# State-space constants: the input table built transposed from a host-transposed B, short-kernel products in four column groups, order and paces reset

## The chip, the cores and the metric

The kernel runs on one core of one Trainium2 chip. The metric is device microseconds of one execution. The kernel before took 1513.43 us, the median of 3 runs (1512.66 to 1515.32).

## The reference

One decoder block: a sequence of 1040 positions (16 learned meta positions and 1024 tokens) of width 1024, float32 throughout.

```python
p     = h @ w_in + b_in            # [u_s5 | q | k | v | o | i | f | g_s5 | g_m]
y_s5  = GLU(GELU(S5(u_s5)))        # grouped complex-diagonal state space
y_m   = (o * HeadNorm(mLSTM(q, k, v, i, f))) @ m_w_out
mix   = sigmoid(g_s5) * y_s5 + sigmoid(g_m) * y_m
h     = LN(alpha * h + mix @ w_o)
h     = LN(alpha * h + relu(h @ w_up + b_up)^2 @ w_down)
...
def _s5_mixer(u, lam_re, lam_im, log_dt, b_re, b_im, c_re, c_im, d_skip):
    lam_bar = jnp.exp(lam * dt)                       # 32 groups x 64 states, complex
    b_bar = ((lam_bar - 1.0) / lam)[..., None] * b_mat
    bu = jnp.einsum("gph,blgh->blgp", b_bar, u)       # 16 inputs per group
    _, state = lax.associative_scan(_linear_recurrence_combine, (a, bu), axis=1)
    y = jnp.real(jnp.einsum("ghp,blgp->blgh", c_mat, state))
    return y + d_skip * u
```

## The kernel before

**Tiling and jobs.** The projection is cut into jobs, one per block of columns of `w_in`, run in the order of the string `ORDER` (`q`/`k`, `v`, `u` for the state space, `o`, and pairs of gate blocks in two parts, `a` and `b`), and then eight `glu` and eight `ym` jobs; the output projection and the feed-forward stage come after all of these. A float32 product is made of three products of rounded parts (`whi`/`wlo` for weights, `hT_hi`/`hT_lo` for activations, lines L262 to L264 in `mm3`); the split is one ScalarE copy (`whi`) and one VectorE subtraction (`wlo`, L243).

**Lanes.** Everything that is not a projection is written as generators: the mLSTM (`ml`), the state-space constants (`s5c`) and batches (`s5`), its GELU (`s5g`), the preparation of gate and up weights (`hg`, `up`), the reload of `hT` (`ah`). After every second term, `mm3` advances a modelled clock (`pump`), and a lane runs on once its last `yield`, times its `PACE`, is past. The lists `ML`, `NL`, `C5`, `K5`, `Z5`, `D5`, `W5` and `Y5` are such yields, for each head or batch. This gives each instruction its place; the scheduler then fixes the order on each engine. All big tiles share one pool of 30 slots, and the small products share three PSUM buffers (`sdps`).

**mLSTM.** Four heads of nine chunks. Per chunk: `pk` (transpose, L517), `pS` (L522, then `sw` on VectorE, L524), `pn` (L532 and L533, numerator and denominator, which reads the state `C`), `pu` (L536, the update, added to `C` on VectorE at L541, copied at L539 for the first chunk), and the normalisation with `dd` (L551 to L554) and `hst`/`hmv`.

**State space.** Chunks of 8 positions, 32 groups, handled in four batches of eight groups. `s5_pre` starts at the job `S5_START` and makes `lam_bar`, its powers `E` (and `ER`, the same in reversed order), the factor `wr`, `wi` and from it `bb`, and the rotation table. When a `u` job ends, it stores `u` to DRAM (L612) and adds two generators. `s5_consts` (for batch b):

- six GpSimd products (L777 and on) of `bb` and `ER` into the table `s5P`, with partitions over states;
- six VectorE operations of `C` and `E` into `s5Rr`, `s5Ri`, and a block-diagonal copy of `bb` beside it;
- eight TensorE transposes of `s5P` (L814) and two ScalarE copies into `s5Mi` (L815), the weights of the input product;
- the short kernel (the response within a chunk): eight products of 32 columns of weights with 128 moving columns (L821, L822), all into partitions 0 to 31 of one PSUM buffer, copied to `s5Kt` (32 x 512), with the skip term added by four small VectorE operations (L826);
- `s5RS` by GpSimd copies; `s5Mx` cleared and filled by 16 DMAs from `s5Kt`, SBUF to SBUF (L839); the table `s5T` by rotation.

`s5_batch` loads `s5U` (eight DMAs, L860), waits for the constants, makes the input products `s5z` (L876), a scan on VectorE in three sets of operations that end with `s5w` (L920), and the output products `s5y`, alternately from `s5Mx` (L931) and from `s5RS` and `s5w` (L932). Loads and stores of this part go through SP's queue, in the order of the program.

**Other places the text speaks of.** The head output `hmF` (L578); the split of gate weights `gmwh` and `gmwl` (L992, L993); the gate sums `hgr` (L970); the stored partial results `gme` (L1152); the reload of a part of `hT` through `ttr` by ScalarE and VectorE (L1103, L1104), with its preparation `tpr` (L1082). `up_early` makes the first up weights and stores them in `wu_dr`. The gate pairs whose `b` part is among the first three (`HOLD`) of `ORDER` and whose `a` part is among the last three keep their weights in SBUF (`HELD`); the others go to DRAM (`gw_dr`, `e_dr`) and come back.

## Time and profile before

The profiled execution is known by its span alone, 1511.4 us from the first to the last instruction; the median of the runs shown is 1513.43.

| engine | busy share of 40 equal slices, in tenths |
|---|---|
| PE | 9999999999999999999999999999999999999997 |
| DVE | 7677756787978785575876676666666689767786 |
| ACT | 7634542425345654241352244444444524433340 |
| POOL | 0000001523104000000000011000000000000000 |
| PE clock | 9999999999999999999999999999999999999999 |
| DMA | 9504362406748678898872257544443997767642 |

A digit is the busy share of one slice of 37.8 us, 9 standing for 90% or more. PE is TensorE's matmuls, PEld its weight loads, DVE VectorE, ACT ScalarE, POOL GpSimd, SP the engine that issues most DMAs. The state-space constants are made in the slices where GpSimd is busy, roughly 230 to 480 us. The core moves 307.06 MB in all, at 203 GB/s.

A row of grouped instructions names line, engine, operation, output and inputs, the count, and then the shortest, median and longest (or total and mean) time of one. A row of the chain or the timeline begins with its start and its length in us. A row of waits names who waited, for whom, and the sum, count and longest.

### The profile page before, as it was taken

The page shows a single profiled execution, that of the slowest core. Times are in us where ns is not written, and L with a number is a line of the kernel's source. Part 1 is how long each engine was busy: PE and PEld are TensorE (multiplying, and loading weights), DVE is VectorE, ACT ScalarE, POOL GpSimd, SP SyncE. Part 2 cuts the span into 40 slices and gives each one's busy share as a digit, 9 for nine tenths or more (in the row PEclk, how much of TensorE's full clock was granted, in tenths as well). Part 3 has the DMA queues.
Part 4 walks back from the last instruction along what each step waited for, and adds up shares of the span by engine and source line. Part 5 has one row for each costly group of instructions (what it writes and reads, how often), then busy time and mean ns, then how long its engine had stood idle before and what let it go on. Part 6 is the DMA issues. An engine that isn't in the chain of part 4 may idle for free.

```text
span 1511.4 us, 20671 instructions
## 1 busy us (share of the span) xinstructions
PE 1495.8 (99%) x7564; PEld 1265.8 (84%) x7564; DVE 1074.7 (71%) x1983; ACT 635.8 (42%) x989; POOL 95.2 (6%) x170
## 2 busy tenths in 40 slices
PE   9999999999999999999999999999999999999997
PEld 9999989998788788888888888888888888888886
DVE  7677756787978785575876676666666689767786
ACT  7634542425345654241352244444444524433340
POOL 0000001523104000000000011000000000000000
PEclk9999999999999999999999999999999999999999
DMA  9504362406748678898872257544443997767642
GB/s 328 156 14 135 110 198 88 145 5 179 247 142 284 184 280 323 342 384 338 340 281 84 71 188 232 180 152 153 144 144 124 313 381 269 241 224 240 205 178 101
DMA packets 150644, 307.06 MB, mean 203 GB/s; under 512 B 19640, under 2 KB 62080, under 8 KB 150544
## 3 DMA queue, kind: packets, MB, share of 16 engines
q1 hardware_dynamic: 147456, 294.68, 56.6%
q0 software_dynamic: 3024, 11.01, 2.3%
q8 instruction: 59, 0.97, 0.3%
q14 instruction: 41, 0.34, 0.1%
q10 hardware_dynamic: 64, 0.07, 0.0%
HBM read 201.63 MB, written 102.90 MB: 201 GB/s over the span
## 4 chain that ended last, share of the span: by engine, by line
PE 93%; DVE 2%; DMA 2%; ACT 1%; POOL 1%; issue 1%; SPq 0%; DVEq 0%; POOLq 0%; ACTq 0%
PE mm L262 22%; PE mm L264 22%; PE mm L263 22%; PE sd L262 6%; PE sd L263 6%; PE sd L264 6%; PE mm L258 2%; DMA wraw<-in_wf_dram 1%; PE pu L536 1%; PE pn L532 1%; PE mm L297 1%; PE pn L533 1%; PE s5y L932 0%; DMA ttr<-t_dr 0%; PE ln L1621 0%
## 5 line engine op out<-in xcount | busy, mean ns | idle before, releaser
L262 PE MATMUL mm<-hT_hi,whi 128*128 128x512 f32 (+3 forms) x400 | 147.7, 369 | 0.0
L264 PE MATMUL mm<-hT_hi,wlo 128*128 128x512 f32 (+3 forms) x400 | 145.5, 365 | 0.0
L263 PE MATMUL mm<-hT_lo,whi 128*128 128x512 f32 (+3 forms) x400 | 144.9, 362 | 0.0
L263 PE MATMUL sd<-dwl,dah 128*128 128x512 f32 (+1 forms) x256 | 98.9, 386 | 0.0
L262 PE MATMUL sd<-dwh,dah 128*128 128x512 f32 (+1 forms) x256 | 98.8, 387 | 0.0
L264 PE MATMUL sd<-dwh,dal 128*128 128x512 f32 (+1 forms) x256 | 98.6, 386 | 0.0
L1829 ACT ACTIVATE dah<-da 128x1024 fp32r<-128x1024 f32 x56 | 58.6, 1052 | 90.6 <-PE sd L263 39.9
L1833 ACT ACTIVATE dwh<-wdr 128x1024 fp32r<-128x1024 f32 x56 | 58.9, 1053 | 77.9 <-DMA wdr<-in_wdn_dram 27.5
L1830 DVE TENSOR_TENSOR dal<-da,dah 128x1024 fp32r<-128x1024 f32 x56 | 68.2, 1220 | 23.1 <-ACT dah L1829 22.8
L262 PEld LDWEIGHTS mm<-hT_hi,whi 128*128 128x128 f32 x400 | 75.2, 188 | 9.7 <-issue 0.3
L263 PEld LDWEIGHTS mm<-hT_lo,whi 128*128 128x128 f32 x400 | 75.2, 188 | 9.3 <-issue 0.3
L264 PEld LDWEIGHTS mm<-hT_hi,wlo 128*128 128x128 f32 x400 | 75.2, 188 | 9.1
L263 PE MATMUL mm<-dwl,dah 128*128 128x512 f32 (+1 forms) x208 | 80.1, 386 | 0.0
L262 PE MATMUL mm<-dwh,dah 128*128 128x512 f32 (+1 forms) x208 | 80.0, 386 | 0.0
L264 PE MATMUL mm<-dwh,dal 128*128 128x512 f32 (+1 forms) x208 | 79.9, 385 | 0.0
L262 PE MATMUL mm<-hT_hi,gmwh 128*128 128x512 f32 x192 | 77.1, 404 | 1.7 <-ACT gme L1152 1.2
L263 PE MATMUL mm<-hT_lo,gmwh 128*128 128x512 f32 x192 | 75.9, 395 | 0.0
L1834 DVE TENSOR_TENSOR dwl<-wdr,dwh 128x1024 fp32r<-128x1024 f32 x56 | 68.2, 1220 | 9.8 <-ACT dwh L1833 9.1
L264 PE MATMUL mm<-hT_hi,gmwl 128*128 128x512 f32 x192 | 74.8, 396 | 0.0
L262 PE MATMUL mm<-whi,hT_hi 128*128 128x256 f32 (+1 forms) x256 | 74.3, 290 | 0.0
L264 PE MATMUL mm<-whi,hT_lo 128*128 128x256 f32 (+1 forms) x256 | 73.9, 289 | 0.0
L263 PE MATMUL mm<-wlo,hT_hi 128*128 128x256 f32 (+1 forms) x256 | 73.6, 288 | 0.0
(492 smaller groups left out, 3967.5 us busy)
## 6 DMA issues: line engine op xcount, KB each, us to landing
da<-act_dr SPq DMA_DIRECT2D x56, 512.0 KB, 5.1
wdr<-in_wdn_dram SPq DMA_DIRECT2D x56, 512.0 KB, 5.5
wraw<-in_wf_dram SPq DMA_DIRECT2D x36, 512.0 KB, 5.9
wur<-in_wup_dram SPq DMA_DIRECT2D x32, 512.0 KB, 4.4
act_dr<-upy SPq DMA_DIRECT2D x64, 256.0 KB, 2.6
wu_dr<-wpre SPq DMA_DIRECT2D x21, 512.0 KB, 4.8
wpre<-wu_dr POOLq DMA_DIRECT2D x21, 512.0 KB, 4.7
act_dr<-upx SPq DMA_DIRECT2D x32, 256.0 KB, 3.4
```

What stands on the lines that cost most here:

```text
L258: t_.matmul(ps, tm[i], tm[j], start=(w == 0 and k == 0), stop=(w == 2 and k == n - 1))
L262: t_.matmul(ps, ah, bh, start=(i == 0 and part[0]), stop=False, skip_group_check=skip)
L263: t_.matmul(ps, ah, bl, start=False, stop=False, skip_group_check=skip)
L264: t_.matmul(ps, al, bh, start=False, stop=(i == n - 1 and part[1]), skip_group_check=skip)
L297: t_.matmul(ps[:, :P], job.first[:, k * P:(k + 1) * P], HF[c0 // P][:, k * P:(k + 1) * P], start=(k == 0), stop=(k == KT - 1))
L532: t_.matmul(pn[:, :257], qi[:, c0:c0 + n], Cs[c][:, :257], start=True, stop=False)
L533: t_.matmul(pn[:, :257], sws[c], vt[c][:, :257], start=False, stop=True)
L536: t_.matmul(pu[:, :257], kws[c][:n], vt[c][:n, :257], start=True, stop=True)
L1829: a_.activation(ah[:, :D], a[:, :D], AF.Copy)
L1830: v_.tensor_tensor(alo[:, :D], a[:, :D], f32(ah[:, :D]), op=OP.subtract)
L1833: a_.activation(wh, raw[i], AF.Copy)
L1834: v_.tensor_tensor(wl, raw[i], f32(wh), op=OP.subtract)
```

## The change

**The input table.** The host passes B a second time, transposed and repeated eight times, so that its partitions are (position in the chunk, input) and its columns (group, state): `s5bt`. `s5_pre` makes the powers times the factor (`WE`, eight powers), transposes these two 128 x 128 blocks once, and stores them in DRAM (`we_dr`). For each batch, `s5_in_load` loads the batch's part of `s5bt` (512 KB, `s5BT`) and, with eight DMAs that repeat a row over 16 partitions, the powers (`s5WT`); four VectorE products and two sums give `s5Mi` in the layout in which TensorE needs it. The six GpSimd products, `ER`, the eight transposes and the two ScalarE copies of each batch are gone.

**The short kernel.** The eight products go to four column groups (partitions 0 to 31, 32 to 63, 64 to 95, 96 to 127), the four of the real part first and then the four of the imaginary part. `s5Kt` is 128 x 128; the skip term is one VectorE operation. It is stored in DRAM (`kt_dr`) and read back into `s5Mx` by eight DMAs.

**Order and paces.** `ORDER`, `S5_START`, `LANE_AT`, `TPW`, `PACE` and seven of the lists of yields have other values. In `ORDER` the `b` parts begin with 11, 10 and 5, so gate pair 9 isn't held in SBUF.

```diff
-ORDER = 'q0 q1 v0 v1 q3 q2 o1 o3 o0 v2 o2 u0 u1 v3 o5 u2 o7 o4 a5 a6 a4 o6 u3 a7 a8 a11 a10 a9 b10 b11 b9 b5 b8 b6 b4 b7'
+ORDER = 'q0 q1 v0 v1 q3 q2 o3 o1 v2 o2 u0 u1 v3 o0 o7 o5 u2 o4 o6 a4 a6 a5 u3 a7 a8 a11 a10 a9 b11 b10 b5 b9 b8 b6 b4 b7'
-TPW = 10.0
-S5_START = 'o2'
-LANE_AT = {'t_prep': 'q3', 'hm_gate': 'b9', 'ah_scale': 'glu2', 'up_early': 'ym2'}
-PACE = {'ml': 0.56, 'cv': 0.093, 's5': 1.0, 's5c': 0.722, 's5g': 2.2, 'ah': 1.569, 'up': 1.036, 'hg': 3.426}
+TPW = 9.77
+S5_START = 'q3'
+LANE_AT = {'t_prep': 'q1', 'hm_gate': 'b9', 'ah_scale': 'glu2', 'up_early': 'ym3'}
+PACE = {'ml': 0.448, 'cv': 0.116, 's5': 1.0, 's5c': 0.65, 's5g': 2.2, 'ah': 1.569, 'up': 1.295, 'hg': 3.426}
-ML = [2.875, 1.694, 2.242, 5.174]
-NL = [0.292, 2.653, 1.274, 3.476]
-C5 = [1.146, 1.058, 1.99, 0.152]
-K5 = [0.475, 9.599, 1.568, 8.674]
+ML = [2.875, 1.694, 2.646, 5.174]
+NL = [0.292, 1.327, 1.274, 6.604]
+C5 = [2.292, 1.058, 1.99, 0.179]
+K5 = [0.475, 9.877, 2.195, 8.674]
-D5 = [3.696, 1.28, 0.645, 0.254]
-W5 = [3.774, 0.829, 4.498, 0.851]
-Y5 = [2.738, 0.964, 2.648, 4.789]
+D5 = [3.696, 1.28, 1.29, 0.254]
+W5 = [3.774, 0.829, 5.308, 0.851]
+Y5 = [2.738, 1.147, 3.707, 4.789]
...
-        dtl = mid.tile([32, 16], F32, name="s5_d")
+        dtl = mid.tile([P, 4], F32, name="s5_d")
-        eye = mid.tile([32, 16], F32, name="s5_eye")
+        eye = mid.tile([P, 16], F32, name="s5_eye")
-        v_.tensor_tensor(eye, ident[:32, 0:16], ident[:32, 16:32], op=OP.add)
+        v_.tensor_reduce(eye, ident.rearrange("p (m h) -> p h m", h=16), axis=mybir.AxisListType.X, op=OP.add)
...
-        ER = es[:, 288:544].rearrange("p (r e q) -> p r e q", r=2, q=16)
+        WE = es[:, 288:544].rearrange("p (r e q) -> p r e q", r=2, q=16)
-        S5.update(E=E, ER=ER, r8=r8)
...
+        yield 1.3
+        sh = [P, 8, 16]
+        cmul(v_, WE[:, 0], WE[:, 1], E[:, 0, 0:8], E[:, 1, 0:8],
+             wr[:, None, :].to_broadcast(sh), wi[:, None, :].to_broadcast(sh),
+             tm[:, 0:128].rearrange("p (a b) -> p a b", b=16), tm[:, 256:384].rearrange("p (a b) -> p a b", b=16))
+        yield 1.3
+        ps = sdps("s5p")
+        for ri in range(2):
+            t_.transpose(ps[:, ri * P:(ri + 1) * P], es[:, 288 + ri * P:288 + (ri + 1) * P], ident)
+        wet = slot("s5wt")
+        a_.activation(wet[:, 0:256], ps[:, 0:256], AF.Copy)
+        nc.sync.dma_start(we_dr.rearrange("p r c -> p (r c)"), wet[:, 0:256])
...
+    we_dr = dram.tile([P, 2, P], F32, name="we_dr")
+    kt_dr = dram.tile([4, P, P], F32, name="kt_dr")
+    def s5_in_load(b):
+        bt, wt = slot("s5BT"), slot("s5WT")
+        nc.sync.dma_start(bt[:, 0:1024], s5bt[:, b])
+        for j in range(8):
+            nc.sync.dma_start(wt[16 * j:16 * j + 16, 0:1024],
+                              bass.AP(tensor=we_dr.tensor, offset=we_dr.offset + ((7 - j) * 16 + 4 * b) * 256,
+                                      ap=[[0, 16], [1, 1024]]))
+        return bt, wt
-        E, ER = S5["E"], S5["ER"]
+        E = S5["E"]
+        bt, wt = s5_in_load(b)
...
-        Pt, tm = slot("s5P"), slot("s5tm")
-        sh = [P, 4, 8, 16]
-        br, bi = (B4(r)[:, :, None, :].to_broadcast(sh) for r in (0, 1))
-        er, ei = (E4(ER, r)[:, :, :, None].to_broadcast(sh) for r in (0, 1))
-        t1, t2 = v4(tm[:, 0:512]), v4(tm[:, 512:1024])
-        pr, pi = v4(Pt[:, 0:512]), v4(Pt[:, 512:1024])
-        g_.tensor_tensor(t1, br, er, op=OP.mult)
-        g_.tensor_tensor(t2, bi, ei, op=OP.mult)
-        yield C5[b]
-        g_.tensor_tensor(pr, t1, t2, op=OP.subtract)
-        g_.tensor_tensor(t1, br, ei, op=OP.mult)
-        yield C5[b]
-        g_.tensor_tensor(t2, bi, er, op=OP.mult)
-        g_.tensor_tensor(pi, t1, t2, op=OP.add)
-        yield C5[b]
-        Mi, Kt = slot("s5Mi"), slot("s5Kt")[:32, :512]
-        for ri in range(2):
-            ps = sdps("s5p")
+        Mi, tm = slot("s5Mi"), slot("s5tm")
+        def v5(t):
+            return t[:, 0:1024].rearrange("p (q r c) -> p q r c", q=4, r=2)
+        def m5(r):
+            return Mi[:, 0:1024].rearrange("p (q g r n) -> p q g r n", q=4, g=2, r=2)[:, :, :, r, :]
+        def t5(r):
+            return v5(tm)[:, :, r, :].rearrange("p q (g n) -> p q g n", g=2)
+        v_.tensor_tensor(tm[:, 0:1024], bt[:, 0:1024], wt[:, 0:1024], op=OP.mult)
+        yield C5[b]
+        v_.tensor_tensor(m5(0), t5(0), t5(1), op=OP.subtract)
+        yield C5[b]
+        v_.tensor_tensor(v5(tm)[:, :, 0], v5(bt)[:, :, 0], v5(wt)[:, :, 1], op=OP.mult)
+        v_.tensor_tensor(v5(tm)[:, :, 1], v5(bt)[:, :, 1], v5(wt)[:, :, 0], op=OP.mult)
+        yield C5[b]
+        v_.tensor_tensor(m5(1), t5(0), t5(1), op=OP.add)
+        yield C5[b]
+        Kt = slot("s5Kt")[:, :P]
+        ps = sdps("s5k")
+        for ri, R in ((0, Rr), (1, Ri)):
-                t_.transpose(ps[:, q * P:(q + 1) * P], Pt[:, ri * 512 + q * P:ri * 512 + (q + 1) * P], ident)
-            a_.activation(Mi[:, 0:1024].rearrange("p (g r s) -> p g r s", g=8, r=2)[:, :, ri, :],
-                          ps.rearrange("p (g s) -> p g s", g=8), AF.Copy)
-            yield C5[b]
-        ps = sdps("s5k")
-        for q in range(4):
-            o = ps[:32, q * P:(q + 1) * P]
-            t_.matmul(o, Rr[:, 576 + q * 32:576 + q * 32 + 32], Rr[:, q * 144:q * 144 + P], start=True, stop=False)
-            t_.matmul(o, Rr[:, 704 + q * 32:704 + q * 32 + 32], Ri[:, q * 144:q * 144 + P], start=False, stop=True)
-        a_.activation(Kt, ps[:32, :], AF.Copy)
-        for q in range(4):
-            k0 = Kt[:, q * P:q * P + 16]
-            v_.scalar_tensor_tensor(k0, S5["eye"], S5["d"][:, q0 + q:q0 + q + 1], k0, op0=OP.mult, op1=OP.add)
+                w0 = 576 + 128 * ri + 32 * q
+                t_.matmul(ps[32 * q:32 * q + 32, 0:P], Rr[:, w0:w0 + 32], R[:, q * 144:q * 144 + P],
+                          start=(ri == 0), stop=(ri == 1))
+        a_.activation(Kt, ps[:, 0:P], AF.Copy)
+        v_.scalar_tensor_tensor(Kt[:, 0:16], S5["eye"], S5["d"][:, b:b + 1], Kt[:, 0:16], op0=OP.mult, op1=OP.add)
+        nc.sync.dma_start(kt_dr[b], Kt)
...
-        mx = Mx[:, 0:1024].rearrange("p (q g t) -> p q g t", q=4, g=2)
-        kt = Kt.rearrange("p (q t) -> p q t", q=4)
+        mx = Mx[:, 0:1024].rearrange("p (g t) -> p g t", g=8)
+        kt = kt_dr[b].rearrange("(g h) t -> h g t", h=16)
-            for g2 in range(2):
-                nc.sync.dma_start(mx[16 * j:16 * j + 16, :, g2, 16 * j:P],
-                                  kt[16 * g2:16 * g2 + 16, :, 0:P - 16 * j])
+            nc.sync.dma_start(mx[16 * j:16 * j + 16, :, 16 * j:P], kt[:, :, 0:P - 16 * j])
...
-    g["s5d"] = a["s5_d"][0].reshape(16, 32).T
+    g["s5d"] = a["s5_d"][0].reshape(4, P).T
+    bt = np.stack([a["s5_b_re"][0], a["s5_b_im"][0]], 0).reshape(2, 4, 4, 2, 64, 16)
```

Three places in the order of instructions. The line numbers of the change are those of the changed file.

TensorE, batch 0 of the constants, around the short-kernel products; `s5p` is the transposed table, `s5k` the short kernel, `pn` and `pu` belong to the mLSTM, `mm` to a projection. Before:

```order
L264 MATMUL mm<-whi,hT_lo 128x256
L262 MATMUL mm<-whi,hT_hi 128x256
L263 MATMUL mm<-wlo,hT_hi 128x256
L814 MATMUL s5p<-ident,s5P 128x128 x4
L821 MATMUL s5k<-s5Rr 32x128
L822 MATMUL s5k<-s5Ri,s5Rr 32x128
```

The last two stand four times in turn. With the change:

```order
L262 MATMUL mm<-whi,hT_hi 128x256
L841 MATMUL s5k<-s5Rr 32x128 x4
L841 MATMUL s5k<-s5Ri,s5Rr 32x128 x4
L532 MATMUL pn<-C,qi 128x257
L533 MATMUL pn<-v_2551,sw 128x257
L263 MATMUL mm<-wlo,hT_hi 128x256
L264 MATMUL mm<-whi,hT_lo 128x256
```

The transposes are gone, the eight products go group by group, and a chunk's `pn` follows them, in the midst of a projection's products.

VectorE, batch 0, from the end of the output table (`s5Rr`, `s5Ri`) on; `sw`, `C`, `dd`, `hst` and `hmv` belong to the mLSTM, `mlo` and `v_3381` to the values of the meta positions, `wlo` to the next job's weights. Before:

```order
L796 TENSOR_TENSOR s5Rr<-s5tm 128x576
L797 TENSOR_TENSOR s5tm<-s5bc,s5E 128x576
L799 TENSOR_TENSOR s5tm<-s5bc,s5E 128x576
L800 SCALAR_TENSOR_TENSOR s5Ri<-s5tm 128x576
L524 TENSOR_TENSOR sw<-pS,gB 128x128
L407 TENSOR_TENSOR mlo<-mm,mlo 16x256
L408 TENSOR_TENSOR mlo<-mm,mlo 16x256
L409 TENSOR_TENSOR v_3381<-mlo,bvt 16x256
L539 COPY C<-pu 128x257
L826 SCALAR_TENSOR_TENSOR s5Kt<-s_eye,s_d,s5Kt 32x16 x4
L243 TENSOR_TENSOR wlo<-wraw,whi 128x1024
```

With the change:

```order
L556 BN_STATS hst<-hraw 128x6
L806 TENSOR_TENSOR s5tm<-s5bc,s5E 128x576
L524 TENSOR_TENSOR sw<-pS,gB 128x128
L557 BN_AGGR hmv<-hst 128x2
L807 SCALAR_TENSOR_TENSOR s5Ri<-s5tm 128x576
L551 TENSOR_SCALAR dd<-pn 128x1
L827 TENSOR_TENSOR s5tm<-s5BT,s5WT 128x1024
L552 SCALAR_TENSOR_TENSOR dd<-pn,ecol,dd 128x1
L541 SCALAR_TENSOR_TENSOR C<-C,dec,pu 128x257
L829 TENSOR_TENSOR s5Mi<-s5tm 128x8x64
L554 RECIPROCAL dd<-dd 128x1
L243 TENSOR_TENSOR wlo<-wraw,whi 128x1024
```

The first multiply of the new table (L827), which reads the nine new loads, stands ahead of a chunk's `dd` and of the update of `C`.

SP's queue, batch 0, from the store of `u` on; `hm_dr` holds a head's output, `wraw` the next job's weights. Before:

```order
L612 DMA us_dr<-uT 128x1040
L860 DMA s5U<-us_dr 16x8x130 x8
L581 DMA hm_dr<-hmF 128x1024 x2
L612 DMA us_dr<-uT 128x1040
L224 DMA wraw<-in_wf_dram 128x1024
L839 DMA s5Mx<-s5Kt 16x4x128 x2
L839 DMA s5Mx<-s5Kt 16x4x112 x2
```

With the change:

```order
L612 DMA us_dr<-uT 128x1040
L877 DMA s5U<-us_dr 16x8x130 x8
L770 DMA s5BT<-in_s5bt_dram 128x1024
L772 DMA s5WT<-we_dr 16x1024 x8
L224 DMA wraw<-in_wf_dram 128x1024
L612 DMA us_dr<-uT 128x1040
L845 DMA kt_dr<-s5Kt 128x128
L857 DMA s5Mx<-kt_dr 16x8x128
L857 DMA s5Mx<-kt_dr 16x8x112
```

The loads of the table stand right behind those of `s5U`, and the short kernel passes through DRAM; the fillings of `s5Mx` go on down to 16 columns, in 16 DMAs before and 8 now.

More of the change, by code (lines that the diff above doesn't have):

```diff
@@ L140, in decoder_block @@
     x, meta, ln0, wf, bf, wv0, wv, bv, bif, conv, wglu, mng, wmo, wo, ln1, ln1r, wup, bup, wdn, ln2r, ln0r,
-    s5l, s5b, s5c, s5d, out,
+    s5l, s5b, s5c, s5d, s5bt, out,
 ):
@@ L709, in s5_pre @@
         yield 1.3
-        for j in range(8):
-            g_.tensor_copy(ER[:, :, j], E[:, :, 7 - j])
         nr, wr, wi, inv = t16("nr"), t16("wr"), t16("wi"), t16("inv")
```

5 lines of the change are left out of this document (4 added, 1 removed).

## The prediction

> **What bounds the kernel now.** I read the page's busy lines first, then the list of what TensorE waited for, then the rows of the operations that the change touches.
>
> ```profile
> span 1511.4 us, 20671 instructions
> PE 1495.8 (99%) x7564; PEld 1265.8 (84%) x7564; DVE 1074.7 (71%) x1983; ACT 635.8 (42%) x989; POOL 95.2 (6%) x170
> ```
>
> TensorE is busy 99% of the span. A microsecond comes off the end only if it comes off TensorE's own stream or off one of its waits. The change works in the stage from about 250 to 500 us, and there the waits are these:
>
> ```profile
> PE mm L262 <- ACT gme L1152: 1.2, 1, 1.2
> PE s5y L932 <- DVE s5w L920: 1.0, 1, 1.0
> PE mm L262 <- ACT gmwh L992: 0.6, 1, 0.6
> PE s5z L876 <- ACT kw L519: 0.2, 1, 0.2
> PE pn L532 <- ACT hmF L578: 0.2, 1, 0.2
> PE s5k L821 <- ACT s5Mi L815: 0.2, 1, 0.2
> ...
> 250.00:500.00 250.00, 246.49 (x1422) 216.26 (x1421) 197.29 (x502) 111.53 (x177) 74.67 (x110) 1.00 0.48 158
> ```
>
> The waits of these 250 us sum to 3.4 us, and TensorE is idle for 3.5 of them. The last row's columns are stretch, sum, then busy time of PE, PEld, DVE, ACT and POOL, granted clock, DMA share and GB/s. The clock is 1.00. VectorE is busy 197 of 250 us, so it has 21% to spare, and GpSimd, from which the change takes work, has 70%.
>
> **The transposes.** Each of the four batches transposes its table with eight TensorE transposes; the change leaves two in all, in the preparation.
>
> ```profile
> L814 PE MATMUL s5p<-ident,s5P x32: 270/272/330, 287.0 to 476.5; 128*128 128x128 f32 x32
> ...
> 287.03 0.60 PE L814 MATMUL s5p<-ident,s5P 128*128 128x128 f32 x4
> 287.46 0.27 PE L517 MATMUL pk<-ident,kT 128*128 128x128 f32 x1
> ```
>
> The 272 ns of a record hold its tail, which lies under the next. What one costs the stream is the distance of the starts: four begin at 287.03 and the next product at 287.46, so 0.43 / 4 = 0.108 us. Thirty fewer are 30 x 0.108 = **3.2 us less**. Nothing hides that, as the engine has no idle time around them.
>
> **The short-kernel products.** Eight per batch (L821 and L822), each 32 columns of weights against 128 moving columns.
>
> ```profile
> L821 PE MATMUL s5k<-s5Rr x32: 269/273/297, 293.8 to 478.4; 128*32 128x128 f32 x32
> ...
> 293.76 0.41 PE L821 MATMUL s5k<-s5Rr 128*32 128x128 f32 x2
> 294.00 0.38 PE L822 MATMUL s5k<-s5Ri,s5Rr 128*32 128x128 f32 x2
> 294.22 0.38 PE L821 MATMUL s5k<-s5Rr 128*32 128x128 f32 x2
> ...
> 295.31 0.38 PE L822 MATMUL s5k<-s5Ri,s5Rr 128*32 128x128 f32 x2
> 295.63 0.70 PE L536 MATMUL pu<-v,kw 16*128 16x257 f32 x2
> ```
>
> L821 issues 16 products and has 32 records, so a product is two records. A pair takes 0.22 us from start to start, a record 0.11, eight pairs 1.76. Now all write partitions 0 to 31, one column group. The change sends four successive products to four groups, and no row here shows two groups at work together. The bounds: if nothing overlaps, no gain; if all four run at once, two rounds of 0.22, a gain of (1.76 - 0.44) x 4 = 5.3 us; and below nothing, if each change of group cost what entering the shape costs now. That is 0.10 us of the gap between 295.31 + 0.22 and 295.63; 32 times it is 3.2 us lost. I take the value between: the two records of one product stay on one group and start in turn, 0.11 apart as now, and the next product's first record goes beside the second. A product then costs one record: 8 x 0.11 + 0.11 = 0.99 per batch, (1.76 - 0.99) x 4 = **3.1 us less**. It needs the weights loaded in time:
>
> ```profile
> 293.76 0.14 PEld L821 LDWEIGHTS s5k<-s5Rr 128*32 128x32 f32 x2 [0.17 <-issue]
> 293.90 0.22 PEld L822 LDWEIGHTS s5k<-s5Ri,s5Rr 128*32 128x32 f32 x2
> ```
>
> The first two loads end 0.14 us after the first began, 0.03 more than one load of 0.11, and the next begins at 293.90, inside the matmul records that run from 293.76 for 0.41. Loads are not what paces these products. The Trainium skill ("TensorE: Matmul & The Clock Gate", Part 3, The mechanism) says the opposite for this case: a load overlaps running matmuls only when the row group differs, and here all four groups use all rows; by that rule this term would be nought, while the two rows just quoted show a load inside a matmul of the same rows.
>
> **The wait for `s5w`.** The last scan of a batch runs on VectorE between its last `s5z` product and its first L932 product, while TensorE does other work. Batch 1 is the one that waited:
>
> ```profile
> 373.92 0.46 PE s5z L876 x4
> ...
> 375.67 1.22 DVE s5w L891
> ...
> 388.47 0.70 DVE s5w L920
> 389.17 0.04 issue
> 389.21 0.49 PE s5y L932 x2
> ```
>
> The chain took 389.21 - 374.38 = 14.8 us. Between the two places the order of before holds 52 products of 0.23 us and few others, 13.3 us in all; the changed order holds 54 of 0.23, 18 of 0.18 and six 257-column products of 0.43 (start distances in this trace), 19.0 us. The cover grows past the chain, so I take this **1.0 us off**. The other batches keep 19 to 25 us. The other 2.4 us of waits sit where ScalarE and VectorE reload `hT`; the order there is nearly that of before, so I keep them.
>
> **What VectorE and the queues take over.** The multiply of B by the table moves from GpSimd to VectorE.
>
> ```profile
> L777 POOL TENSOR_TENSOR s5tm<-s5bb,s5E 128x512 f32<-128x512 f32 x4 | 5.4, 1351 | 63.9 <-DMA gw_dr<-wraw 47.7 <-PE s5y L932 16.2
> L1082 DVE TENSOR_TENSOR tpr<-tpr 128x512 f32<-128x512 f32 x4 | 2.8, 690 | 0.0
> L970 DVE TENSOR_TENSOR hgr<-hgr,hgo x8: 1214/1215/1224, 538.2 to 618.0; 128x1024 f32<-128x1024 f32 x8
> L815 ACT ACTIVATE s5Mi<-s5p 128x512 f32<-128x512 f32 x8 | 4.7, 593 | 8.4 <-PE s5p L814 8.4
> ```
>
> GpSimd loses 24 of about 1.35 us, ScalarE eight of 0.59; VectorE gains 1.22 + 4 x 0.69 = 4.0 us per batch, 16 in all, beside its 53 us of slack. As work that costs nothing; as work at the head of a queue it can cost. Each batch's first multiply waits for nine new loads, and a VectorE instruction that waits holds all behind it: in batch 0 the state update `C` (L541) of the mLSTM, on which TensorE's next `pn` depends; in batch 3 the split of `gmwl`. When do the loads land?
>
> ```profile
> 276.78 0.32 SPq L612 DMA_DIRECT2D us_dr<-uT  x1
> 280.05 3.64 SPq L860 DMA_DIRECT2D s5U<-us_dr  x8
> ...
> s5U<-us_dr SPq DMA_DIRECT2D x32, 65.0 KB, 3.2
> wraw<-in_wf_dram SPq DMA_DIRECT2D x36, 512.0 KB, 5.9
> ttr<-t_dr SPq DMA_DIRECT2D x8, 512.0 KB, 8.0
> ```
>
> After `u` of batch 0 is stored at 276.8, its eight loads occupy SP until 283.7. `s5BT` (512 KB, like `wraw`) follows and lands 5.9 us on, at 289.6; the eight `s5WT` (64 KB, like `s5U`) take 3.6 us to issue and 3.2 to land, 290.5 or, if the eighth has to wait for `s5BT`, 292.8. That is 14 to 16 us after the store. In the changed order about 13 us of TensorE work (the stream from the end of `u0` to the `pn` ahead of it) lie between the same two places, so VectorE stands 1 to 3 us, and TensorE's cover behind (the update is used some 5 us of stream later) takes most of it. In batch 3 the cover is about as thin; batches 1 and 2 have more. Bounds: nothing, and 3 us for each of these two. I take **1.5 us more** in all. The round trip of `Kt` through DRAM hides under 34 to 67 us of stream that the order leaves between the `s5k` products and the first use of `Mx`; without that cover it would cost a store and a load, some 6 us. Six more 512 KB transfers for gate pair 9, now outside the held three, go beside a DMA share of 0.48. Starting the preparation at q3 puts its roughly one hundred small operations beside 50 us stretches with VectorE busy 34 to 37; the two transposes stand about 3 us of stream behind the last of them. `up_early` starts a job later but ends ahead of the same two products; `wu_dr` is read long after. Both at nothing; a thin cover would show as a wait there of 1 to 3 us.
>
> **The sum.** -3.2 - 3.1 - 1.0 + 1.5 = -5.8 us: a span of 1505.6. The profiled execution's span is 1511.4; the median of the runs shown is 1513.4, 2.0 more, which I take as what lies around the span. Forecast: 1507.6 us, 0.4% faster.
>
> **The rivals.**
> 1. *The groups do not overlap*, so the change does not do what it says: -3.2 - 1.0 + 1.5 = -2.7, 1510.7. For it: no row shows two groups at once. Against it: the load rows above. It is also where the skill's rule on loads ends. A loss on every change of group would end at 1513.9.
> 2. *VectorE stuck behind the loads*, the slower end. If the path to DRAM is as slow as the `ttr` row, 8.0 us for `s5BT`, and the eighth `s5WT` waits for it and lands 3.2 later, the multiply starts 11 us after SP's issue, with six `s5tm`/`s5Rr` operations of about 0.75, 4.5 us, ahead of it. VectorE then stands 6.5 us, and where TensorE's next product needs what is queued behind, it stands nearly as long: three batches x 6 = 18, less 7.3 gained, 1524; with half of it covered 1515 to 1518. It decides from a TensorE wait of 2.6 us per batch (10.3 us over four), where 0.2% slower begins. For it: VectorE's 79% and the SP queue in order. Against it: the same engine reads `gB` after DMAs now, and TensorE shows no wait for that.
> 3. *All overlaps and the old waits go too*: -3.2 - 5.3 - 3.4 = -11.9, 1501.5; with the new waits 1503. For it: the mLSTM's last head ends some 45 us of stream earlier, so VectorE is freer where the 1.2 and 0.6 waits sit.
> 4. *The moved order gives back what is gained*: waits of 4 to 8 us more anywhere in 50 to 500 us, 1511 to 1516.
>
> **How the numbers follow.** 0.2% (3.0 us) is about what a measurement of this kernel can tell from no change; faster begins below 1510.4, slower above 1516.5. Forecast, 1503.5 to 1510: 0.51. Rival 1: 0.16, of which 0.04 below 1510.4. Rival 2: 0.14. Rival 3: 0.15. Rival 4: 0.04. Faster 0.51 + 0.15 + 0.04 = 0.70, within 0.16, slower 0.14. The range of 1501.5 to 1517 leaves out the far half of rival 2 and a part of rival 3, under 2 in 10.
>
> **What would show it.** Thirty records of `s5p` fewer. Eight `s5k` products in about 1.0 us from first start to the next product: 1.76 says rival 1, 0.44 full overlap. No wait for `s5w` in TensorE's list. VectorE's wait for `s5WT` or `s5BT` in its own list: a few us in all, and rows "PE pn" or "PE mm" released by VectorE under 2 us; more is rival 2. POOL near 50 us busy. The forecast is wrong if TensorE's waits between 50 and 500 us sum to over 10 us, or if the span after 550 us changes in length, since nothing there is meant to move.

## The result, and the profile after

The changed kernel takes 1519.12 us (median of 5 runs, 1518.07 to 1519.68), the kernel before 1513.43 (5 runs, 1512.17 to 1515.32). The ratio is 1.0038, 95% interval 1.0025 to 1.005: slower by 0.4%, where 0.4% faster was forecast, and 2.1 us beyond the range. In two of the runs below one execution took more than twice as long (3451 and 3814 us); the ratios leave it out.

The page of the kernel after, its busy lines; the columns are those of before:

```profile
span 1517.1 us, 20633 instructions
PE 1491.3 (98%) x7534; PEld 1260.2 (83%) x7534; DVE 1079.1 (71%) x1997; ACT 634.8 (42%) x985; POOL 63.7 (4%) x138
```

The span grew by 5.7 us while TensorE's busy time fell by 4.5. So the time went into waits, and some of the busy time is slow work. TensorE's list of waits, after:

```profile
PE mm L264 <- DVE gmwl L1010: 6.0, 1, 6.0
PE pS L522 <- DVE sw L524: 3.3, 1, 3.3
...
PE pk L517 <- ACT kw L519: 1.3, 1, 1.3
...
PE mm L262 <- ACT gme L1169: 0.3, 1, 0.3
...
PE s5y L949 <- DVE s5w L937: 0.3, 1, 0.3
```

Two pauses stand out. The waits for `kw` and `sw` lie near 125 us, the wait for a gate split `gmwl` near 478 us. Before, no pause behind TensorE's first instruction was longer than 1.2 us. The waits that the prediction named in the stage did shrink: `s5w` 1.0 to 0.3, `gme` 1.2 to 0.3, `gmwh` 0.6 to none in the list. Between 50 and 500 us TensorE is idle for 12.4 us in all, where it was 4.4.

The two pauses by the windows view of the kernel after (stretch, length, busy time of PE, PEld, DVE, ACT, POOL, granted clock, DMA share, GB/s):

```profile
123.00:127.00 4.00, 1.81 (x12) 1.29 (x10) 2.70 (x7) 2.71 (x3) 1.76 (x1) 1.00 0.97 315
127.00:129.50 2.50, 0.06 (x1) 0.07 (x1) 2.50 (x9) 0.22 (x1) 0.63 (x2) 0.60 0.79 191
129.50:134.00 4.50, 4.50 (x14) 4.13 (x15) 4.39 (x27) 0.93 (x3) 0.00 (x0) 0.50 0.25 63
134.00:138.00 4.00, 4.00 (x23) 3.91 (x22) 3.59 (x17) 2.27 (x4) 0.00 (x0) 0.96 1.00 257
478.00:482.00 4.00, 0.17 (x1) 0.00 (x0) 3.93 (x6) 0.00 (x0) 2.83 (x3) 1.00 0.97 386
482.00:484.00 2.00, 0.00 (x0) 0.00 (x0) 2.00 (x3) 0.91 (x2) 0.00 (x0) 0.62 0.98 375
484.00:489.50 5.50, 5.32 (x13) 4.21 (x14) 5.50 (x10) 3.79 (x6) 0.00 (x0) 0.52 1.02 404
489.50:493.00 3.50, 3.50 (x17) 2.84 (x16) 1.79 (x3) 1.08 (x3) 0.68 (x4) 1.00 0.51 158
```

The granted clock is 0.50 for 6.8 us around each, and TensorE works through 4.9 and 5.1 us of that at half speed. So each pause is paid again by some 2.5 us: 1.3 + 3.3 + 2.45 = 7.1 for the first, 6.0 + 2.55 = 8.6 for the second, 15.7 in all.

Against that stands a gain larger than forecast. TensorE's timeline at the short kernel of batch 0, after (start, length):

```profile
304.45 0.43 PE L841 MATMUL s5k<-s5Rr 128*32 128x128 f32 x8
304.69 0.40 PE L841 MATMUL s5k<-s5Ri,s5Rr 128*32 128x128 f32 x8
305.02 0.70 PE L532 MATMUL pn<-C,qi 128*128 128x257 f32 x2
```

From the first product to the next instruction it is 0.57 us, where it was 1.87; over the four batches that is 5.1 us less. With 3.2 of transposes (the prediction's estimate) and 2.2 of waits gone, 15.7 - 10.5 = 5.2; the span measured 5.7 more.

**What holds up the first pause.** The chain of the mLSTM's first gates, in the timelines of VectorE, ScalarE and GpSimd after; the brackets hold the idle time ahead and what ended it:

```profile
111.99 0.17 DVE L623 TENSOR_SCALAR s_t<-s_lam 128x16 f32<-128x16 f32 x1 [3.19 <-DMA s_lam<-in_s5l_dram]
121.19 2.19 DVE L503 SCALAR_TENSOR_TENSOR gB<-gB,acol,mask 128x128 f32<-128x128 f32 x8 [2.50 <-DMA gB<-grow_dr]
125.17 0.17 DVE L509 COPY dec<-wiB 128x9 f32<-128x9 f32 x1 [1.30 <-DMA wiB<-wrow_dr]
125.27 3.40 DVE L243 TENSOR_TENSOR wlo<-wraw,whi 128x1024 fp32r<-128x1024 f32 x1
129.11 0.27 DVE L524 TENSOR_TENSOR sw<-pS,gB 128x128 f32<-128x128 f32 x1
...
125.24 2.35 POOL L508 TENSOR_TENSOR qi<-qT,wiB 128x1024 f32<-128x1024 f32 x1 [42.04 <-PE pk L517]
```

The chain runs from the gate transposes on TensorE at 107.0 us to `sw` at 129.4, 22 us. Its longest piece is the load of `wiB`, 8.8 us; before, it took 8.6. In the new order only 17.8 us of TensorE work stand between these transposes and the second chunk's scores `pS`; the old order had 26.8 (from start to start in the two traces, less the idle time; the expectations below count 16 and 25). At its end, `dec` waits at the head of VectorE for a load, and the split `wlo` takes 3.40 us, where the same shape takes 1.2 elsewhere, because GpSimd's `qi` runs beside it.

**What holds up the second.** The timelines of VectorE and GpSimd after:

```profile
472.87 0.76 DVE L807 SCALAR_TENSOR_TENSOR s5Ri<-s5tm 128x576 f32<-128x576 f32 x1
475.18 1.23 DVE L827 TENSOR_TENSOR s5tm<-s5BT,s5WT 128x1024 f32<-128x1024 f32 x1 [1.55 <-DMA s5WT<-we_dr]
476.44 0.98 DVE L829 TENSOR_TENSOR s5Mi<-s5tm 128x512 f32<-128x512 f32 x1
477.45 0.98 DVE L831 TENSOR_TENSOR s5tm<-s5BT,s5WT 128x512 f32<-128x512 f32 x1
478.36 1.09 DVE L832 TENSOR_TENSOR s5tm<-s5BT,s5WT 128x512 f32<-128x512 f32 x1
479.49 0.98 DVE L834 TENSOR_TENSOR s5Mi<-s5tm 128x512 f32<-128x512 f32 x1
480.39 0.68 DVE L1446 TENSOR_TENSOR wus<-wraw 128x512 f32<-128x512 f32 x1
...
482.92 1.22 DVE L1010 TENSOR_TENSOR gmwl<-wraw,gmwh 128x1024 fp32r<-128x1024 f32 x1
...
475.60 2.30 POOL L849 COPY s5RS<-s5Rr 64x512 f32<-64x512 f32 x2 [7.37 <-PE mm L263]
477.95 1.98 POOL L849 COPY s5RS<-s5Ri 64x512 f32<-64x512 f32 x2
```

Batch 3's table stands ahead of the split that TensorE waits for: 1.6 us of waiting for `s5WT` and 5.3 us of work, 6.9 in all. Behind it come four weight sums of the up weights (2.5 us), and then the split. Four of the five operations take about 1 us here; in the other three batches they take 0.66 to 0.69, as forecast. Here they run beside GpSimd's copies into `s5RS`, and each ends 0.54 us after one of these copies.

### The profile page after: what moved, and what is told of

It reads as the page before. It is cut to its first block, busy times and chain, and to the rows that moved or that the text cites. A ratio compares the mean times of both kernels' runs of the same rounds, so it can differ in the third digit from the quotient of the medians.

```text
span 1517.1 us, 20633 instructions
## 1 busy us (share of the span) xinstructions
PE 1491.3 (98%) x7534; PEld 1260.2 (83%) x7534; DVE 1079.1 (71%) x1997; ACT 634.8 (42%) x985; POOL 63.7 (4%) x138
## 4 chain that ended last, share of the span: by engine, by line
PE 73%; issue 10%; DVE 8%; DMA 5%; ACT 2%; SPq 1%; POOL 0%; DVEq 0%; POOLq 0%; ACTq 0%
PE mm L262 17%; PE mm L264 17%; PE mm L263 17%; PE sd L263 6%; PE sd L262 6%; PE sd L264 6%; DVE cy L358 2%; DMA wiB<-wrow_dr 1%; DMA tpr<-h_dr 1%; DVE wlo L243 1%; PE pn L532 1%; PE pu L536 1%; PE pn L533 1%; DMA h_dr<-hf 1%; DMA wpre<-wu_dr 1%
```

## The experiments

Every run was timed against the kernel before on the same chip. The ratios, with 95% intervals:

| run | median us | ratio to before |
|---|---|---|
| old_code_new_tables | 1545.45 | 1.0214 [1.02, 1.0228] |
| new_code_old_tables | 1544.68 | 1.0214 [1.02, 1.0228] |
| before_with_groups | 1518.26 | 1.0035 [1.0022, 1.0047] |
| after_ml_pace_back | 1531.01 | 1.0119 [1.0105, 1.0133] |
| after_lam_own_buffer | 1518.75 | 1.0039 [1.0027, 1.0051] |
| after_dec_on_gpsimd | 1514.6 | 1.0016 [1.0007, 1.0026] |
| after_table3_last | 1523.25 | 1.0071 [1.0059, 1.0083] |
| after_table3_early | 1532.15 | 1.0129 [1.0116, 1.0142] |
| after_both_edits | 1522.25 | 1.0062 [1.0049, 1.0075] |
| after_table3_first | 1527.57 | 1.0098 [1.0084, 1.0112] |
| after_dec_table3_first | 1525.38 | 1.0076 [1.0064, 1.0089] |
| dec_o6_behind_a7 | 1519.79 | 1.0044 [1.0028, 1.0059] |
| dec_o6_behind_u3 | 1525.76 | 1.008 [1.0066, 1.0094] |
| dec_one_wt_load | 1518.95 | 1.0043 [1.003, 1.0056] |
| dec_without_table3 | 1515.95 | 1.0011 [1.0002, 1.0019] |
| dec_without_table3_and_loads | 1513.47 | 0.9997 [0.9988, 1.0006] |
| dec_table3_on_gpsimd | 1519.29 | 1.0038 [1.0025, 1.005] |
| before_dec_on_gpsimd | 1517.29 | 1.0028 [1.0017, 1.0039] |

**Tables and code apart.** First the order string, paces and yields (the tables) of the change in the code of before, and the other way round.

```diff
-ORDER = 'q0 q1 v0 v1 q3 q2 o1 o3 o0 v2 ... (and the other tables of before)
+ORDER = 'q0 q1 v0 v1 q3 q2 o3 o1 v2 o2 ... (and the other tables of the change)
```

> The code of before (table on GpSimd with eight transposes a batch, short kernel in one column group) with the order string, paces and yields of the change. Theory: the loss comes from two pauses of TensorE, each followed by some 5 us at half clock; the one near 125 us comes from the new order and paces alone (the mLSTM's first chunks stand 16 us of TensorE work behind the gate transposes, where they stood 25), the one near 478 us from the table on VectorE. Then the first pause is here (some 5 us of waits and 2.4 us of slow clock), the second is not, and nothing is gained in the stream: 1513.4 + 7.4 - 1.0 (wait for s5w) = about 1520 us. Rival, that the new code is to blame for both pauses: 1512 to 1513 us and no pause near 125 us. Rival, that order and paces are to blame for both: about 1527 us, with both pauses.

> The code of the change with the order string, paces and yields of before. Theory: the stream is 8.4 us shorter (3.2 for transposes, 5.2 for the short kernel in four groups) and the pause near 125 us is gone, as the gate chain has its 25 us of cover back; where VectorE now makes the table of batch 3 ahead of a gate split, a pause of up to 6 us and 2.6 us of slow clock stays. 1513.4 - 8.4 = 1505 us without that pause, up to 1514 with it. Rival, that the new code brings the pause near 125 us: 1512 or more with a wait of sw or kw there.

TensorE's timeline of the old code with the new tables shows the first pause at the same place, nearly of the same size:

```profile
126.28 0.33 PE L517 MATMUL pk<-ident,kT 128*128 128x128 f32 x1 [1.96 <-ACT kw L519]
130.62 0.79 PE L522 MATMUL pS<-qT,kT 128*128 128x128 f32 x2 [3.13 <-DVE sw L524]
```

So the first pause comes with the tables; the new code with the old tables doesn't have it. The totals were wrong, though, by 25 us and by 31 or more. Old code and new tables also has a wait of 7.4 us for `gmwl`, so a wait at that split isn't proof of the new table's work: there the old table's six GpSimd products run beside VectorE (477 to 486 us), and VectorE operations of 0.69 us ahead of the split take 1.6 to 1.8. New code and old tables has pauses of 9.4 us at 344 us, for the normalisation, and of 8.0 at 500, again for `gmwl`. Neither set of tables suits the other code.

**The short kernel alone.** The edit is the short-kernel part of the diff above, in the kernel before.

> The kernel before with the short-kernel part alone changed: four column groups, the response stored to DRAM and read back into s5Mx; table, transposes, order and paces stay. Theory (the four groups run at once, 0.57 us from the first product to the next instruction where it was 1.87): 4 x 1.3 = 5.2 us less, 1508.2 us. By the prediction's own term (a product costs one record) 3.1 us less, 1510.3. If the way through DRAM is not covered: a wait of s5y for s5Mx, and 1512 or more.

The products start as in the change, 7 ns apart in a group of four, and the order holds 5.1 us less TensorE work. The time rose all the same, above all three forecasts: TensorE's list has `pk` on `C` 2.6 (before none), `gme` 2.5 (1.2), `sw` 1.3 (none), and half clock lasts 3.4 us. There is no wait for `s5Mx`. The 5.1 us are real, but TensorE only comes earlier to what it waits for.

**The first pause.** One pace back, then two edits of single places:

```diff
-PACE = {'ml': 0.448, ...
+PACE = {'ml': 0.56, ...
```

> The changed kernel with one number back: the pace of the mLSTM lane, 0.448 to 0.56. That puts 21.7 us of TensorE work between the gate transposes and the second chunk's scores, where the change has 16.2. Theory, that this cover is what the pause near 125 us lacks: the gate chain of about 23 us leaves 1 to 2 us of wait, the clock stays at full, and the time falls by 5 to 7 us, to 1512 to 1514, with the wait near 478 us as it moves. Rival, that the wait of VectorE for s_lam (3.2 us) alone makes the pause: it stays above 3 us and so does the slow clock, 1517 or more.

A miss: 1531. The wait near 125 us fell from 4.6 to 2.8 us and half clock followed it all the same, and three more pauses of 2.1 to 2.8 us opened behind (337, 486 and 510 us).

```diff
-        lam = mid.tile([P, 112], F32, tag="row", bufs=1, name="s5_lam")[:, :48]...
+        lam = mid.tile([P, 48], F32, name="s5_lam")...
```

> The changed kernel with one edit: s_lam gets a buffer of its own, so that its load and the small VectorE operations behind it no longer wait for the gate row of the mLSTM and stand before the gate chain, not inside it. Theory, that the pause near 125 us is a chain that is too long for its cover (23 us against 16 to 20 of TensorE work): without the 3.2 us that VectorE waits for s_lam, the waits for kw and sw fall from 4.6 us to under 2 and the half clock behind them goes: 1519.1 - 2.6 - 2.4 = about 1514 us. Rival, that the loads of wiB and gB (8.8 us under way beside the hT reload's transfers) set it: the pause stays near 4 us, 1518 or more. The pause near 478 us stays in both.

The rival was right. VectorE no longer waits for `s_lam`, the wait for `kw` is gone, that for `sw` stays at 3.4 us. The small operations moved into the first 60 us and opened waits of 1.0 and 1.6 us there. And this pause, longer than the changed kernel's, was not followed by half clock (windows of that run):

```profile
127.00:131.00 4.00, 0.56 (x5) 0.27 (x3) 4.00 (x5) 0.42 (x2) 2.08 (x2) 1.00 0.87 232
131.00:135.00 4.00, 4.00 (x24) 3.84 (x24) 3.03 (x9) 0.48 (x2) 0.00 (x0) 1.00 0.54 153
```

```diff
-        v_.tensor_copy(dec[:, 0:9], wiB[:, META - 1:LEN:P])
+        g_.tensor_copy(dec[:, 0:9], wiB[:, META - 1:LEN:P])
```

> The changed kernel with one instruction moved: the copy of the decays (dec from wiB) goes from VectorE to GpSimd, behind qi, which waits for the same load. Theory: near 125 us VectorE waits 1.3 us for wiB at this copy, and the split wlo behind it then takes 3.4 us beside GpSimd's qi where it takes 1.2 elsewhere; both stand ahead of sw. With the copy away, wlo and sw are done before wiB lands; the wait for sw (3.3 us) and the half clock behind it (2.4 us) go: 1519.1 - 5 = about 1514 us. Rival: sw itself is held while qi runs (2.4 us), the wait stays at 2 us or more and the half clock may stay: 1517 or more. The pause near 478 us stays in both.

1514.6 is the theory's time, but its mechanism came only in part. The timelines of VectorE and GpSimd in that run:

```profile
123.69 1.21 DVE L243 TENSOR_TENSOR wlo<-wraw,whi 128x1024 fp32r<-128x1024 f32 x1
124.83 2.35 DVE L628 SCALAR_TENSOR_TENSOR s_t<-s_t,s_t 128x16 f32<-128x16 f32 x1
...
127.57 0.28 DVE L524 TENSOR_TENSOR sw<-pS,gB 128x128 f32<-128x128 f32 x1
...
124.68 2.47 POOL L508 TENSOR_TENSOR qi<-qT,wiB 128x1024 f32<-128x1024 f32 x1 [42.13 <-DMA wiB<-wrow_dr]
```

`wlo` takes 1.21 us again, ahead of `qi`. The rival was right in part: an operation of 16 columns (0.17 us elsewhere) now takes 2.35 beside `qi`, so the chain is only 0.9 us shorter. Waits of 1.8 us for `kw` and 2.1 for `sw` are left, 3.9 where it was 4.6, and half clock lasted 3.4 us, not 6.8. That is 1.5 us at this place, of 3.2 between the two profiled spans and 4.5 between the medians; where the rest comes from was not traced. The eleven executions themselves lie 5.3 us apart, with mean granted clocks of 0.993 to 0.997.

> The kernel before with the copy of the decays on GpSimd alone. Theory: the mLSTM's first chunks have 25 us of cover there and TensorE shows no wait, so the same edit that took 4.5 us off the changed kernel takes nothing here: within 1 us of 1513.4. Rival, that the hold of VectorE costs something elsewhere too: 1 to 3 us less.

A miss: the same edit in the kernel before costs 0.28%. TensorE's list there shows

```profile
PE s5y L932 <- DVE s5w L920: 4.7, 1, 4.7
```

where it was 1.0. The edit moves one copy per head, four in all, and the last one does this. GpSimd stands 8.8 us at that copy, for the load of `wiB`, until 372.2 us. The products for `s5P` behind it, which were done by 369.5 us before, now run with `qi` beside batch 1's scan: three `s5w` operations of 0.69 us take 1.59, 1.78 and 2.88 us on VectorE. From `s5z` to the first L932 product it takes 18.5 us, where the prediction's chain has 14.8.

**The second pause: moving the table of batch 3.** To the end of its batch, to the end of batch 2, to the front, and combined with an edit of the first pause:

```diff
+        if b == 3:
+            yield from table()
         S5["m", b] = (RS, Mi, Mx, T)
```

> The changed kernel with one edit: the five VectorE operations of batch 3's table are issued at the end of that batch's constants and no longer ahead of the gate split that TensorE waits for. Its loads stay where they are. Theory, that the pause of 6.0 us near 478 is VectorE's 1.6 us of waiting for s5WT and 5.3 us of table work: the wait falls to under 1 us, the half clock behind it (2.7 us) goes, and the time is 1519.1 - 8 = about 1511 us, if the table does not come too late for s5z of batch 3. Rival, that VectorE's other work, the weight sums, or late weight loads hold the split: 1516 or more, with the wait for gmwl above 3 us.

> The changed kernel with batch 3's table, its nine loads too, made right behind the constants of batch 2, some 30 us earlier. Theory (as for the table at the end): the wait for gmwl near 478 us falls below 1 us and its half clock goes, and SP's queue is free of the eight s5WT issues (5.5 us) ahead of the weight loads: about 1511 us; if VectorE is as full there (it is busy 10 of 10 us at 450 to 460), the pause only moves, and the time stays at 1516 to 1520 with a wait for gmwl, gmo or s5w earlier.

> The changed kernel with both edits, the own buffer of s_lam and batch 3's table last. Theory: the two pauses are independent and the two gains add: 1519.1 - 5 - 8 = about 1506 us, faster than before by 0.5%, which is what the shorter stream was worth. Rival, that a pause removed early lets TensorE run into a later one (VectorE is what paces 450 to 500 us): only the smaller part of the second gain is seen, 1510 to 1514 us.

> The changed kernel with batch 3's table (nine loads, five VectorE operations) made right behind the preparation, near 220 to 280 us, where VectorE is busy about half of the time. Theory: from u3 on VectorE paces the stage (52.6 us of its work in 57.3 us, TensorE's own is 48.6), so only work taken out of the stage shortens it; 5.3 us of table and 1.6 of waiting leave it, the wait of 6.0 us and its half clock of 2.7 go down to at most 2 us in all: about 1511 to 1513 us. Rival, as with the table at the end of the batch, that the waits turn up at the next split or sum (gme, gmo): 1516 or more. A risk: two buffers are held for 200 us.

> Both edits together. Theory: the two pauses are independent, the gains add: 1519.1 - 5 - 7 = about 1507 us, 0.4% faster than before. Rival: what the first gives is lost at the second, since VectorE paces the later stage: 1511 to 1513 us.

All five theories missed, by 12 to 21 us; of the rivals, that of the table in front came true (waits at the next split or sum, 1516 or more). The wait for `gmwl` fell to 1.9 us or less, but others came. TensorE's list with the table at the end:

```profile
PE mm L262 <- ACT gme L1177: 6.8, 2, 4.3
...
PE mm L264 <- DVE gmwl L1018: 1.4, 1, 1.4
```

In the early place a wait for `gmo` of 4.4 us came at 460 us; in front, `wlo` waits of 3.4 us in all, the longest at 685 us. (The figures of 52.6 and 48.6 us in these expectations add up record lengths, which overlap; by the windows view VectorE was busy 48.6 of the 57.3 us from `u3` on, and 45.5 of 52.8 before.)

**The second pause: work left out, cover added, one load.** All three groups build on the copy of the decays on GpSimd.

```diff
-            v_.tensor_tensor(tm[:, 0:1024], bt[:, 0:1024], wt[:, 0:1024], op=OP.mult)
... (the five operations, for b == 3)
+            a_.activation(Mi[:, 0:1024], bt[:, 0:1024], AF.Copy)
```

> The changed kernel with dec on GpSimd, and without the five VectorE operations of batch 3's table: ScalarE copies the loaded B into its place, so the input products of batch 3 have unscaled weights (this part of the computation is left out); the nine loads stay. Theory, that the pause near 478 us is these operations and the wait ahead of them (6.9 us in all) in a stage that VectorE paces: the wait for gmwl falls under 1 us, the half clock goes, and nothing comes in their place: 1514.6 - 8.5 = about 1506 us. Rival, that the stage's other VectorE work (46 us without the table against 48.6 us of TensorE's) still holds a split, or that the weight loads are late behind the eight s5WT issues: waits for gmwl, gmo or gme of 3 us or more, 1510 to 1514 us.

> The changed kernel with dec on GpSimd, and without batch 3's table: neither its nine loads nor its five VectorE operations are there, GpSimd writes zeros in its place (this part of the computation is left out). Theory, that VectorE's operations and the loads ahead of the weight loads make the whole pause near 478 us: no wait over 1.5 us and no half clock there, 1514.6 - 8.7 = about 1506 us; the table of batch 3 has then cost what its transposes (0.9 us a batch) and short kernel (1.3 us a batch) gave over all four batches. Rival, that the stage waits for other traffic (DMA engines busy 0.9 of the time): a wait for gmwh or gme of 2 us or more, 1510 us or more.

Both theories missed. ScalarE copies the loaded powers too in the first of these runs. Without the operations the wait for `gmwl` is gone, but 2.8 us for the next split's `gmwh` come, which ScalarE reaches behind a wait of 4.8 us for the reload of `hT` (`ttr`), and 6.8 us of half clock: 1515.95. Without the loads too, that place is free. TensorE's list, and the windows at 478 us of that run:

```profile
PE mm L262 <- ACT gme L1175: 3.2, 3, 2.7
PE pk L517 <- ACT kw L519: 2.1, 1, 2.1
PE pS L522 <- DVE sw L524: 2.1, 1, 2.1
...
478.00:482.00 4.00, 4.00 (x19) 3.23 (x18) 4.00 (x7) 2.33 (x3) 0.00 (x0) 1.00 0.98 327
```

From the end of `u3` to the last `s5z` it takes 81.0 us there, 83.7 with the loads left in, 84.9 in the changed kernel with and without the moved copy, and 81.1 before. So batch 3's table and its loads make the whole second pause. But a wait for `gme` at 496 us, 2.7 us with 3.4 of half clock, takes 4.4 us back, as the rival said. And the first pause is still there: 4.2 us of waits (`kw` and `sw` in the list) and 6.8 us of half clock behind them, which cost another 2.6. So the time is 1513.5, not 1506. Behind the same first pause, half clock lasted 3.4 us with the copy moved alone, 6.8 here, and none in the run that leaves the loads in (3.0 us of waits).

```diff
-... u2 o4 o6 a4 a6 a5 u3 a7 a8 a11 ...
+... u2 o4 a4 a6 a5 u3 a7 o6 a8 a11 ...
```

> The changed kernel with dec on GpSimd, and in the order string the job o6 put behind a7, not ahead of a4. The job is some 11 us of TensorE work with one VectorE split of 1.2 us, so the stage from u3 on gets cover that VectorE does not pay for. Theory, that VectorE paces this stage: the pause near 478 us and its half clock go, 1514.6 - 8.5 = about 1506 us, unless the stage that loses the job (400 to 440 us, VectorE busy 8 of 10 us) opens a wait of its own: then 1508 to 1512. Rival, that the splits wait for loads: 1513 or more.

> As the run with o6 behind a7, with o6 right behind u3. The cover then lies where VectorE makes the first part of batch 3's constants. Theory: the same 1506 us, as it is the cover of the stage that counts and not its place. Rival, that it must lie between the first gate split and the table: the pause stays at half, 1510 us.

Both missed. Behind `a7`, the wait for `gmwl` halved (6.1 to 2.8 us), but half clock still followed it, and waits of 0.7 to 2.0 us opened elsewhere; behind `u3` there are pauses of 4.2, 3.2 and 2.5.

```diff
-        for j in range(8):
-            nc.sync.dma_start(wt[16 * j:16 * j + 16, 0:1024], ...
+        nc.sync.dma_start(wt[:, 0:1024], ... ap=[[16 * 256, 8], [0, 16], [1, 1024]]))
```

> The changed kernel with dec on GpSimd, and with the powers stored once in reversed order, so that one DMA of 512 KB loads s5WT in place of eight of 64 KB; the result is the same. SP issues 8 loads fewer in a row and 28 fewer in all (0.45 to 0.69 us each), so what is queued behind, the weight loads among it, starts some 5 us earlier. Theory, that VectorE's table alone makes the pause near 478 us: it stays at 4 to 6 us, 1511 to 1515. Theory, that the queue and the table make it together: the wait falls to 1 to 3 us, and the time to 1508 to 1511 us.

The time, 1518.95, lies above both forecasts. The wait for `gmwl` stayed at 6.6 us, so SP's eight issues are not what delays it: with the table there, VectorE's operations are.

```diff
+        e_ = g_ if b == 3 else v_
```

> The changed kernel with dec on GpSimd, and the five table operations of batch 3 on GpSimd, which is idle for most of that stage; loads and order string as in the change. Theory, that GpSimd's two-operand work holds VectorE for its whole time (2.4 us beside qi): 5 operations of 1.4 to 2.5 us are some 8 us, so VectorE loses as much as the 5.3 us that it is spared, and the pause near 478 us stays at 4 us or more: 1513 to 1518 us. Rival, that VectorE runs on beside them: the pause goes as in the run without the table, 1508 to 1511 us.

The time, 1519.29, lies above both forecasts, and the mechanism in between: the wait for `gmwl` fell to 1.4 us, and two `gme` waits of 2 us each came. VectorE and GpSimd in that run:

```profile
477.23 2.05 DVE L1011 TENSOR_TENSOR gmwl<-wraw,gmwh 128x1024 fp32r<-128x1024 f32 x1 [1.28 <-ACT gmwh L1010]
483.66 2.31 DVE L1122 TENSOR_TENSOR hT_lo<-ttr,hT_hi 128x1024 fp32r<-128x1024 f32 x1
...
475.44 2.77 POOL L828 TENSOR_TENSOR s5tm<-s5BT,s5WT 128x1024 f32<-128x1024 f32 x1 [7.42 <-DVE wraw L1449]
483.10 1.79 POOL L835 TENSOR_TENSOR s5Mi<-s5tm 128x512 f32<-128x512 f32 x1
```

Splits that take 1.22 us alone take 2.05 and 2.31 beside GpSimd. Each ends 1.08 us after the GpSimd operation that was running when it was issued. GpSimd's five operations cost 9.3 us of its time, and VectorE part of that.

## Why the prediction was wrong

- **The transposes**: right. There are 30 records fewer; the 3.2 us are the distance of their starts before, and no run leaves them out alone.
- **The short-kernel products**: the direction was right, the size was off. The term said 3.1 us (one record per product); it measured 5.1, close to the upper bound of 5.3. Four products start 7 ns apart, and both records of a product overlap with those of the other groups. The Trainium skill's rule on loads (TensorE: Matmul & The Clock Gate, Part 3, The mechanism), by which a load overlaps running matmuls only where the row groups differ, does not hold here: all four groups use all rows, and the four ran at once, 1.87 / 0.57 = 3.3 times as fast. The Trainium skill's table of packings (the same page, Part 3, Measured speedup vs the span model), which the prediction left out, gives 2.38 times for three column groups; the trace sides with the table.
- **The wait for `s5w`**: right, 1.0 to 0.3; rival 3's hope for `gme` and `gmwh` came true too.
- **"As work that costs nothing"**: the first step that failed. VectorE's "53 us of slack" is a mean over 250 us. Where batch 3's table was put, VectorE had no idle time between 475.2 and 484.2 us, and the five operations stood in front of a split that TensorE needed from 478.2 on. The place was named ("in batch 3 the split of `gmwl`"), but bounded at 3 us, by the wait for the loads alone; the operations behind the wait weren't added. They also took 5.3 us there rather than the 4.0 of the prediction, as GpSimd's copies ran beside them. Leaving out the operations and loads took the pause away. VectorE's wait for `s5WT` itself was as forecast: 1.6 us, twice.
- **Batch 0**, the other place named, cost nothing: VectorE waited 1.6 us for `s5WT`, and TensorE's list has no wait between 284 and 310 us.
- **"Starting the preparation at q3 ... Both at nothing"**: the second step that failed, and it is wider than that sentence. The text asked what the new tables do to the state-space work and not what they do to the mLSTM's first gates, whose cover they cut from 26.8 to 17.8 us. The old code with the new tables shows this pause at its place, so the tables cause it. By its own waits it is 4.6 us. Which piece of the chain makes it is not settled: without the wait for `s_lam` 3.4 us stayed, with the copy moved 3.9, with the old pace 2.8.
- **The price of a pause**: a wait was priced at its length. Here a wait of 3.3 or 6.0 us also brought half clock, 2.5 us more each. That is a third of the loss, and no term of the prediction held it. How much half clock a pause brings is in part luck, as the last section shows.
- **Rival 4** (the moved order gives back what is gained) is the one that happened, with both pauses, at 15.7 us rather than its 4 to 8; it had a chance of 0.04. Rival 2 had the mechanism of the second pause with another cause: VectorE stuck behind its own work rather than behind the loads.
- **The signs**: "TensorE's waits between 50 and 500 us sum to over 10 us" was met, with 12.4 us idle. GpSimd was busy for 63.7 us, not "near 50"; the prediction's own rows give 63 (95.2 less 24 operations of 1.35).
- Almost nothing moved after 550 us, as forecast: from the last `s5z` to the end it is 971.5 us before and 972.6 after.

Two things stay open. Why small edits open new waits of 2 to 7 us far behind them is traced here for two runs, the moved copy in the kernel before and the old code with the new tables (GpSimd beside VectorE), and not for the others. And no version here beats the kernel before: with the copy moved and batch 3's table left out the time is only equal, and that run still has the first pause and a `gme` wait of 2.7 us, both with half clock behind. What the shorter stream is worth without them was not reached.

## What to carry to other kernels

When TensorE is 99% busy, a cut in its stream is worth only what the other engines' chains leave: list for each chain the TensorE work that covers it and the chain's own length, and look for the few whose margin is less than the cut (here 27 us of cover for a chain of 25, and 18 for one of 22 after the change). Work that moves to an engine with slack must be priced at the place where the order puts it, with all of its operations and the wait ahead of them, and what GpSimd runs beside them. A table of paces that was set for one program isn't a neutral part of a change, and isn't to be judged apart from the code: old code with new tables and new code with old ones were each 2.1% slower than the kernel before, where the change is 0.4% slower.
